# The FFN's first product by Strassen's seven products, its weight sums on GpSimd, and h kept in DRAM

## The chip, the cores and the metric

The kernel runs on one core of one Trainium2 chip. The metric is the device time of one execution in microseconds (us). One number counts: the median over the runs of a kernel. Nothing else runs on the core.

## The reference

One layer of a diffusion transformer on 1024 tokens of 1024 features, with 256 context tokens that only give starting states to the scans. Everything is float32.

```python
px = modulate(x, mx[0], mx[1]) @ w_in[l]                    # 1024 x 3840
...
mix_x = token_mixers(px, hg_x, s_f, s_b, *mix_args)
x_new = layer_norm(ALPHA * x + mx[2] * (mix_x @ w_out[l]), ln1_g[l], ln1_b[l])
ffn_x = conv_ffn(modulate(x_new, mx[3], mx[4]), ffn_up[l], ffn_conv_w[l], ffn_conv_b[l], ffn_down[l], rows)
x_new = layer_norm(ALPHA * x_new + mx[5] * ffn_x, ln2_g[l], ln2_b[l])

def conv_ffn(h, w_up, conv_w, conv_b, w_down, grid_rows):
    a, g = jnp.split(h @ w_up, 2, axis=-1)                  # 1024 x 1024 @ 1024 x 5632
    bsz, t, f = a.shape
    a = dwconv3x3(a.reshape(bsz, grid_rows, t // grid_rows, f), conv_w).reshape(bsz, t, f) + conv_b
    return (jax.nn.gelu(a, approximate=False) * g) @ w_down # 2816 x 1024
```

The change is in `h @ w_up` and in what stands around it. The tokens are a grid of 16 rows by 64 columns; `dwconv3x3` is a 3x3 filter with weights of its own for every feature, so it needs all 1024 tokens of a feature of `a`.

## The kernel before

**Matrix products.** Each float32 operand is split into a high part (rounded to float32r by a cast on ScalarE) and a low part (the exact rest, by a subtraction on VectorE): `split`, lines 82 and 83. A product of 128 by 128 by 512 is then three matmuls: high by high, low by high, high by low (`mm3`, lines 102 to 104). Weights are loaded from DRAM by SyncE's queue (SP) in pieces of 128x512 into a ring of four tiles `r` and are split up to 350 instructions ahead of the program's place (`AHEAD`, `load_split`).

**Stages.** Start-up, the token mixers (scan, short convolution, spatial gate), the output projection with the first layer norm (`out_proj`), `ffn_up`, `ffn_down` with the last layer norm. `modulate2` turns the normalised tiles of x_new feature-major: PE transposes into a PSUM bank (tile `psB`, line 933), ScalarE scales and shifts it in the bank (line 935), and `split` makes the high and low parts `x2`. The first half of the tokens is done while `out_proj` still runs. The second half (tiles 4 to 7) comes at the end of it, and `banks_up` lets the first three column blocks of `ffn_up` begin with the first half, so that these products cover the second half's preparation.

**ffn_up** runs over 22 blocks f of 128 features. Block f has two columns of `w_up`: the column f for `a` and the column 22+f for the gate `g`. `up_half` computes 128 features by 512 tokens in one PSUM bank: 8 blocks of features, three matmuls each. So a column takes 48 matmuls and a block f 96. After the two halves of `a`, ScalarE writes the middle tap with the bias (line 953) and a copy of `a` (line 954) to SBUF; VectorE adds the other eight taps, one `scalar_tensor_tensor` each on all 1024 tokens (line 964); ScalarE applies Gelu in place (line 966); VectorE multiplies by the two banks of `g` (line 970). The result `h[f]` stays in SBUF for all 22 blocks, in the tiles `hk` (blocks 0 to 9, room that the scan used) and `h`. In blocks 2 to 9 one column of the last modulation is computed besides (`ada_col`), from which the row `gate5` is made.

**ffn_down** takes two halves of 512 tokens. For each, 22 blocks f of h are split again into high and low parts (`dh`; `dhr` for the first) and multiplied with rows f of `w_down` into all eight PSUM banks.

**What sets the order.** A scheduler puts each engine's instructions into one fixed list, by the program's order and the priorities (`high_priority`). An engine takes its list strictly in turn: an instruction that waits for a semaphore holds up all that stands behind it on its engine. SP's list holds the DMA starts in the same way. GpSimd (POOL) has eight instructions in the whole kernel, all at the start.

## Time and profile before

| | |
|---|---|
| time, median of 2 runs (1353.05 and 1355.92) | 1354.49 us |
| profiled execution: span from first to last instruction | 1354.2 us |
| TensorE busy (PE) | 1319.4 us, 6730 matmuls |
| VectorE busy (DVE) | 945.0 us, 1735 instructions |
| ScalarE busy (ACT) | 472.1 us, 878 instructions |
| GpSimd busy (POOL) | 1.7 us, 8 instructions |
| mean clock granted to TensorE | 0.997 |

For the profiled execution the record holds the span alone, and it lies 0.3 us under the median; the span is taken as the execution's own time. An engine's row gives its busy time, its share of the span and the number of instructions. In a group of instructions stand the line, the engine, the operation, output<-inputs, the shapes, the count, then the busy time in us and the mean in ns of one, then the idle time of the engine just ahead of these instructions with what ended it. In a timeline row stand the start and the length in us. Matmuls overlap in the record: each is listed with 0.39 us though the next begins about 0.23 us later, so the spacing of the starts is what one costs.

### The profile page before, as it was taken

The numbers are of one execution on the slowest core, as the hardware profiler recorded it, in microseconds if no ns is written. First come the engines' busy times: TensorE is split into PE (matmuls) and PEld (weight loads), VectorE is DVE, ScalarE is ACT, GpSimd is POOL, SyncE is SP. The second block draws the span as 40 slices with busy tenths as digits, with TensorE's granted clock in tenths as the row PEclk, the third lists the DMA queues.
The fourth block names the chain that finished last, engine by engine and source line by source line (L and its number), as shares of the span: only waits on it lengthen the run. The fifth ranks groups of instructions, "written<-read, shape, count | busy, mean of one in ns | idle before, by whom it ended". The sixth has DMA issues, their size and how long they took to land.

```text
span 1354.2 us, 17543 instructions
## 1 busy us (share of the span) xinstructions
PE 1319.4 (97%) x6730; PEld 1114.1 (82%) x6730; DVE 945.0 (70%) x1735; ACT 472.1 (35%) x878; POOL 1.7 (0%) x8
## 2 busy tenths in 40 slices
PE   4999999999999999999999999999999999999997
PEld 3888988898888887877888888888888888888885
DVE  7979954869688688886876757575656664349357
ACT  4744544433331424434322222222222233223330
POOL 0000000000000000000000000000000000000000
PEclk9999999999999999999999999999999999999998
DMA  9672410132131444221222111211111033235332
GB/s 331 249 242 77 133 63 31 32 116 81 40 112 60 137 148 156 99 104 62 95 77 78 63 63 47 68 50 54 47 47 47 31 115 135 93 109 201 111 105 82
DMA packets 60900, 135.14 MB, mean 100 GB/s; under 512 B 7168, under 2 KB 7824, under 8 KB 60816
## 3 DMA queue, kind: packets, MB, share of 16 engines
q1 hardware_dynamic: 60816, 134.02, 29.2%
q8 instruction: 53, 0.87, 0.3%
q14 instruction: 31, 0.25, 0.1%
HBM read 125.59 MB, written 8.40 MB: 99 GB/s over the span
## 4 chain that ended last, share of the span: by engine, by line
PE 82%; DVE 9%; DMA 4%; ACT 3%; issue 1%; DVEq 0%; SPq 0%; ACTq 0%
PE psA L102 16%; PE psA L103 16%; PE psA L104 16%; PE psB L103 9%; PE psB L102 9%; PE psB L104 9%; PE psB L575 4%; PE psB L614 1%; DMA r<-in_w_out 1%; DMA cada<-in_ada 1%; DVE adat L172 1%; ACT O L639 1%; DMA adat<-in_ada 1%; DVE bnst L137 1%; DVE wl L83 1%
## 5 line engine op out<-in xcount | busy, mean ns | idle before, releaser
L83 DVE TENSOR_TENSOR wl<-r,wh 128x512 fp32r<-128x512 f32 x160 | 104.3, 687 | 155.8 <-ACT wh L82 149.9
L82 ACT CAST wh<-r 128x512 fp32r<-128x512 f32 x160 | 92.5, 619 | 311.5 <-PE psB L103 160.7
L102 PE MATMUL psA<-x,wh 128*128 128x512 f32 x352 | 137.3, 390 | 0.8 <-ACT x L82 0.8
L104 PE MATMUL psA<-x,wl 128*128 128x512 f32 x352 | 137.2, 390 | 0.0
L103 PE MATMUL psA<-x,wh 128*128 128x512 f32 x352 | 137.2, 390 | 0.0
L102 PE MATMUL psB<-x,wh 128*128 128x512 f32 x352 | 137.0, 389 | 0.0
L104 PE MATMUL psB<-x,wl 128*128 128x512 f32 x352 | 136.9, 389 | 0.0
L103 PE MATMUL psB<-x,wh 128*128 128x512 f32 x352 | 136.9, 389 | 0.0
L102 PE MATMUL psA<-xh,wh 128*128 128x512 f32 x320 | 126.7, 396 | 0.0
L103 PE MATMUL psA<-xl,wh 128*128 128x512 f32 x320 | 126.4, 395 | 0.0
L104 PE MATMUL psA<-xh,wl 128*128 128x512 f32 x320 | 125.8, 393 | 0.0
L964 DVE SCALAR_TENSOR_TENSOR h<-a,par,h 128x945 f32<-128x945 f32 (+2 forms) x96 | 117.4, 1223 | 7.1 <-ACT a L954 4.2
L964 DVE SCALAR_TENSOR_TENSOR hk<-a,par,hk 128x945 f32<-128x945 f32 (+2 forms) x80 | 97.6, 1223 | 5.6 <-ACT a L954 3.4
L102 PEld LDWEIGHTS psA<-x,wh 128*128 128x128 f32 x352 | 66.0, 188 | 14.7 <-ACT x L82 1.2
L102 PEld LDWEIGHTS psB<-x,wh 128*128 128x128 f32 x352 | 66.1, 188 | 13.9 <-DVE x L83 0.3
L103 PEld LDWEIGHTS psB<-x,wh 128*128 128x128 f32 x352 | 66.1, 188 | 13.8
L103 PEld LDWEIGHTS psA<-x,wh 128*128 128x128 f32 x352 | 66.1, 188 | 13.6
L104 PEld LDWEIGHTS psB<-x,wl 128*128 128x128 f32 x352 | 66.1, 188 | 13.6
L104 PEld LDWEIGHTS psA<-x,wl 128*128 128x128 f32 x352 | 66.1, 188 | 13.6
L104 PEld LDWEIGHTS psA<-xh,wl 128*128 128x128 f32 x320 | 60.2, 188 | 11.8
L103 PEld LDWEIGHTS psA<-xl,wh 128*128 128x128 f32 x320 | 60.2, 188 | 11.8 <-issue 0.2
L102 PEld LDWEIGHTS psA<-xh,wh 128*128 128x128 f32 x320 | 60.2, 188 | 11.7 <-issue 0.2
(316 smaller groups left out, 2787.7 us busy)
## 6 DMA issues: line engine op xcount, KB each, us to landing
r<-in_wup SPq DMA_DIRECT2D x88, 256.0 KB, 2.7
r<-in_w_down SPq DMA_DIRECT2D x88, 256.0 KB, 2.9
r<-in_win SPq DMA_DIRECT2D x56, 256.0 KB, 2.8
ada<-in_ada SPq DMA_DIRECT2D x24, 512.0 KB, 3.8
adat<-in_ada SPq DMA_DIRECT2D x16, 512.0 KB, 6.7
r<-in_ada SPq DMA_DIRECT2D x26, 256.0 KB, 3.0
cada<-in_ada SPq DMA_DIRECT2D x11, 512.0 KB, 5.4
x<-in_x SPq DMA_DIRECT2D x8, 512.0 KB, 5.8
```

The costliest lines, as they stand in the source:

```text
L82: nc.scalar.copy(hi, src)
L83: nc.vector.tensor_tensor(out=lo, in0=src, in1=hi.bitcast(F32), op=ALU.subtract)
L102: mm(out, lh, rh, start=first, stop=False)
L103: mm(out, lh, rl, start=False, stop=False)
L104: mm(out, ll, rh, start=False, stop=last)
L137: nc.vector.bn_stats(out=st[:, c, :], in_=x[:, c * 512:(c + 1) * 512])
L172: nc.vector.tensor_tensor_reduce(out=t, in0=t, in1=sc[:, i * n:(i + 1) * n], scale=1.0, scalar=0.0 if i == 0 else acc[:, 0:1], op0=ALU.mul ...
L575: nc.tensor.matmul(b[:, c, :], A[:, t0:t0 + P], strided(kq, 3 * T + t0, [[2 * B, P // (2 * B)], [B - T, 2], [1, B]]), start=c == 0, stop=c ...
L614: nc.tensor.matmul(b[:, c, :], KTt[:, g * 4 + c, :], vt[:, g * 4 + c, hv], start=c == use[g][0], stop=c == use[g][-1])
L639: nc.scalar.activation(O[:, k, :], b[:, c, :], AF.Square, accum_out=ss[:, k:k + 1])
L964: nc.vector.scalar_tensor_tensor(out=o, in0=a3[:, r0 + di:r1 + di, c0 + dj:c1 + dj], scalar=cw(i, j), in1=o, op0=ALU.mult, op1=ALU.add)
```

## The change

**Seven products.** Let X be x2 transposed to features by tokens, cut into halves of features and of tokens, and for a block f let a11, a12 be the upper and lower feature halves of its `a` column and a21, a22 those of its gate column. The four results (a and g, each for both halves of the tokens) come from seven products of 128 by 512 by 512, not eight. Each is 4 blocks of features by three matmuls, so 12 matmuls. They use sums of weights, S1 = a21+a22, S2 = S1-a11, a12-S2, a11-a21, and sums of X, which are made once: the forms "11", "21", "22" are quarters of X, T1 to T4 are sums. Each form and each sum of weights is split into high and low parts of its own.

**Where the sums go.** `weight_form` makes the four sums and all seven low parts of a block on GpSimd, 11 operations of 128x512; the seven casts stay on ScalarE. The raw columns of a block come by two loads of 512 KB into tiles `raw`. Six pieces for the start come by `load_form`.

**A block's results.** Products 1, 6, 7 and 4 add up in one bank (`x`, tag B) and are read out in between: after 1 into `p1`, after 6 into `u2` (both ScalarE), after 7 with `r` on VectorE, after 4 by the multiplication with Gelu's result. Products 2, 5 and 3 go to a pair of neighbouring banks `zv` (tag A, now allotted as two pairs). VectorE adds p1 or u2 to a half of the pair (`a_done`), ScalarE writes the middle tap with the bias back into the bank, and the eight taps accumulate in the pair in PSUM, with `a` read from SBUF.

**Start.** `up_begin` begins blocks 0 to 3 with products of the first token half (72 matmuls: product 1 of blocks 0 to 3, product 2 of 0 and 1), then normalises tiles 4 to 7, transposes 32 pieces into the second halves of the two pairs, and makes the forms; "22" and T3 have their low parts on GpSimd. x_new's first half, modulated, was stored to DRAM (`xr`) and comes back for the sums. Blocks 0 and 1 then go together through products 6, 5, 3, 7, 4; blocks 2 and 3 through the rest of theirs; blocks from 4 on through all seven.

**h in DRAM.** Each block's h is stored to DRAM (`hd`), and `ffn_down` loads it again, 128x512 at a time, into a ring of six tiles `hr`, by SP's queue. The rows `gate5`, `ln2_g` and `ln2_b` are loaded for `ffn_down` too. Small constants and masks move to pools that are given back earlier, and the mixers and `out_proj`, which used single banks of tag A, now get halves of the pairs.

```diff
+    def pair(self):
+        return self.pp.tile([P, 2, 512], F32, tag="A", bufs=2, name=self.name("psA"))
+
     def bank(self, tag="A", shape=(512,)):
+        if tag == "A":
+            if self.half is None:
+                self.half = self.pair()
+                b = self.half[:, 0]
+            else:
+                b, self.half = self.half[:, 1], None
+            return b if len(shape) == 1 else b.rearrange("p (a b) -> p a b", a=shape[0])
         return self.pp.tile([P, *shape], F32, tag=tag, bufs=4, name=self.name("ps" + tag))
...
-    def split(self, src, hi, lo):
+    def split(self, src, hi, lo, on=None):
         nc = self.nc
         nc.scalar.copy(hi, src)
-        nc.vector.tensor_tensor(out=lo, in0=src, in1=hi.bitcast(F32), op=ALU.subtract)
+        (on or nc.vector).tensor_tensor(out=lo, in0=src, in1=hi.bitcast(F32), op=ALU.subtract)
...
+    FORM = {1: "11", 2: "21", 3: "22", 4: "T4", 5: "T1", 6: "T2", 7: "T3"}
...
+    def weight_form(self, u, k):
...
+            if k in (5, 6) and "S1" not in r:
+                r["S1"] = combine(self.Rt(nm="s1"), a21, a22, ALU.add)
+            if k == 6:
+                r["S2"] = combine(self.Rt(nm="s2"), r["S1"], a11, ALU.subtract)
+            if k == 3:
+                combine(a12, a12, r["S2"], ALU.subtract)
+            if k == 7:
+                combine(a21, a11, a21, ALU.subtract)
+            src = {1: a11, 2: a12, 3: a12, 4: a22, 5: r.get("S1"), 6: r.get("S2"), 7: a21}[k]
+            self.split(src, w[:, 0], w[:, 1], pool)
+        return w
+
+    def product(self, k, work):
+        for j in range(4):
+            xh, xl = self.form(self.FORM[k], j)
+            c = slice(j * P, (j + 1) * P)
+            for bank, w, start in work:
+                mm = self.nc.tensor.matmul
+                mm(bank, w[:, 0, c], xh, start=start and j == 0, stop=False, skip_group_check=True)
+                mm(bank, w[:, 0, c], xl, start=False, stop=False, skip_group_check=True)
+                mm(bank, w[:, 1, c], xh, start=False, stop=j == 3, skip_group_check=True)
+
+    def up_begin(self, ys):
...
+        self.product(1, [(us[0].x, w[0], True)])
+        self.product(2, [(us[0].zv[:, 0], w[1], True)])
+        self.product(1, [(us[1].x, w[2], True)])
+        self.product(2, [(us[1].zv[:, 0], w[3], True)])
+        self.product(1, [(us[2].x, w[4], True)])
+        self.product(1, [(us[3].x, w[5], True)])
+        self.norm2(ys)
...
+        def one(j):
+            raw, v, t2 = self.S((2, 512), nm="xraw"), self.S((2, 512), nm="xv"), self.Rt(nm="t2")
+            nc.sync.dma_start(raw, self.xr[j])
+            for i in range(2):
+                self.shift2(us[i].zv[:, 1], ys, j + 4 * i, v[:, i])
+            nc.vector.tensor_tensor(out=raw[:, 0], in0=v[:, 0], in1=raw[:, 0], op=ALU.subtract)
+            nc.vector.tensor_tensor(out=t2, in0=v[:, 1], in1=raw[:, 0], op=ALU.subtract)
+            self.split(t2, *self.form("T2", j))
+            held[j] = raw, v, t2
+
+        def two(j):
+            raw, v, t2 = held.pop(j)
+            self.split(raw[:, 0], *self.form("T1", j))
+            self.split(v[:, 1], *self.form("22", j), nc.gpsimd)
+            nc.vector.tensor_tensor(out=v[:, 0], in0=v[:, 1], in1=v[:, 0], op=ALU.subtract)
+            self.split(v[:, 0], *self.form("T3", j), nc.gpsimd)
+            nc.vector.tensor_tensor(out=raw[:, 1], in0=raw[:, 1], in1=t2, op=ALU.subtract)
+            self.split(raw[:, 1], *self.form("T4", j))
+
+        for f, j in ((one, 0), (one, 1), (two, 0), (one, 2), (two, 1), (one, 3), (two, 2), (two, 3)):
+            f(j)
+        self.begun = us[2:]
+        self.units(us[:2], (6, 5, 3, 7, 4))
...
+        def after(self, k):
...
+            def a_done(g, c):
+                z = self.zv[:, g]
+                nc.vector.tensor_tensor(out=self.a[:, g], in0=z, in1=c, op=ALU.add)
+                nc.scalar.activation(z, self.a[:, g], AF.Identity, scale=cw(1, 1), bias=b.par[:, C_CB + f:C_CB + f + 1])
+
+            if k == 6:
+                nc.scalar.copy(self.u2, self.x)
+                self.a = b.ut("a")
+                a_done(0, self.p1)
+            elif k == 5:
+                self.r = b.ut("r")
+                nc.scalar.copy(self.r[:, 0], self.zv[:, 1])
+            elif k == 3:
+                a_done(1, self.u2)
...
+                        nc.vector.scalar_tensor_tensor(out=o, in0=a3[:, r0 + di:r1 + di, c0 + dj:c1 + dj], scalar=cw(i, j), in1=o,
+                                                       op0=ALU.mult, op1=ALU.add)
+                self.h = b.ut("h")
+                nc.scalar.activation(self.h.rearrange("p g t -> p (g t)"), z, AF.Gelu)
+            elif k == 7:
+                nc.vector.tensor_tensor(out=self.r[:, 1], in0=self.x, in1=self.r[:, 0], op=ALU.add)
+            elif k == 4:
+                for g, m in ((0, self.x), (1, self.r[:, 1])):
+                    nc.vector.tensor_tensor(out=self.h[:, g], in0=self.h[:, g], in1=m, op=ALU.mult)
+                nc.sync.dma_start(b.hd[f], self.h.rearrange("p g t -> p (g t)"))
+
+    def units(self, us, ks):
+        for k in ks:
+            ws = [self.weight_form(u.f, k) for u in us]
+            self.product(k, [(u.open(k), w, k in (1, 2, 5)) for u, w in zip(us, ws)])
+            for u in us:
+                u.after(k)
...
-                with self.tc.high_priority((2 * self.AHEAD, 0, 0)[f] if g == 0 and f < 3 else self.AHEAD):
-                    self.split(self.h[f][:, g * 512:(g + 1) * 512], *hh)
+                with self.tc.high_priority(self.AHEAD):
+                    h = dn.tile([P, 512], F32, tag="hr", bufs=6, name=self.name("hr"))
+                    nc.sync.dma_start(h, self.hd[f][:, g * 512:(g + 1) * 512])
+                    self.split(h, *hh)
```

The fixed lists show the change at three places. GpSimd, where the first column block's weights are made: `x_` are low parts of the forms "22" and T3, `s_` and `raw_` the sums of weights of block 0, `wf_6041` the low part that its product 6 needs. Before, GpSimd had no instruction here.

```order
L95 TENSOR_TENSOR x_816_5775<-xv_5930,x_814_5773 128x512
L95 TENSOR_TENSOR x_820_5779<-xv_5930,x_818_5777 128x512
L95 TENSOR_TENSOR x_816_5775<-xv_5948,x_814_5773 128x512
L95 TENSOR_TENSOR x_820_5779<-xv_5948,x_818_5777 128x512
L95 TENSOR_TENSOR x_817_5776<-xv_5976,x_815_5774 128x512
L95 TENSOR_TENSOR x_821_5780<-xv_5976,x_819_5778 128x512
L997 TENSOR_TENSOR s_6046<-raw_6043 128x512
L997 TENSOR_TENSOR s_6048<-s_6046,raw_6042 128x512
L997 TENSOR_TENSOR raw_6043<-raw_6042,raw_6043 128x512
L997 TENSOR_TENSOR raw_6042<-raw_6042,s_6048 128x512
L95 TENSOR_TENSOR wf_6041<-s_6048,wf_6041 128x512
```

The sums of block 0 stand behind six low parts of forms, and the low part for product 6 behind all four sums.

VectorE, a block's convolution and what stands behind it. Before (one block; `wl` are low parts of weights, the two L970 rows the multiplications of the block ahead):

```order
L970 TENSOR_TENSOR hk_5899<-hk_5899,psB_6109 128x512
L970 TENSOR_TENSOR hk_5899<-hk_5899,psB_6134 128x512
L83 TENSOR_TENSOR wl_6388<-r_6389,wh_6387 128x512
L83 TENSOR_TENSOR wl_6388<-r_6393,wh_6387 128x512
L964 SCALAR_TENSOR_TENSOR hk_5899<-a_6169,par,hk_5899 128x15x63
L964 SCALAR_TENSOR_TENSOR hk_5899<-a_6169,par,hk_5899 128x960
```

And now, the end of blocks 0 and 1 (`psA_5783` and `psA_5784` are their pairs; L1122 is the addition of `r` after product 7, L1125 the multiplications after product 4):

```order
L1117 SCALAR_TENSOR_TENSOR psA_5783<-a_6092,par,psA_5783 128x15x63
L1117 SCALAR_TENSOR_TENSOR psA_5784<-a_6096,par,psA_5784 128x15x63
L1117 SCALAR_TENSOR_TENSOR psA_5783<-a_6092,par,psA_5783 128x960
L1117 SCALAR_TENSOR_TENSOR psA_5784<-a_6096,par,psA_5784 128x960
L1117 SCALAR_TENSOR_TENSOR psA_5783<-a_6092,par,psA_5783 128x15x63
L1117 SCALAR_TENSOR_TENSOR psA_5784<-a_6096,par,psA_5784 128x15x63
L1122 TENSOR_TENSOR r_6129<-psB_5785,r_6129 128x512
L1122 TENSOR_TENSOR r_6131<-psB_5786,r_6131 128x512
L1125 TENSOR_TENSOR h_6175<-h_6175,r_6129 128x512
L1125 TENSOR_TENSOR h_6187<-h_6187,r_6131 128x512
```

The sixteen taps of both blocks take turns, and the additions that read the banks after product 7 stand behind all of them.

SP, where `ffn_up` ends and `ffn_down` begins. Before:

```order
L97 DMA r_8823<-in_wup 128x512
L97 DMA r_8892<-in_wup 128x512
L97 DMA r_8896<-in_wup 128x512
L97 DMA r_8968<-in_w_down 128x512
L97 DMA r_8972<-in_w_down 128x512
L97 DMA r_9006<-in_w_down 128x512
```

And now (`hd_96` is the store of block 21's h, `hr_9123` the first load of block 0's):

```order
L109 DMA r_9113<-in_w_down 128x512
L109 DMA r_9117<-in_w_down 128x512
L1126 DMA hd_94<-h_8780 128x1024
L1126 DMA hd_95<-h_8921 128x1024
L1126 DMA hd_96<-h_9062 128x1024
L1190 DMA hr_9123<-hd_75 128x512
L1190 DMA hr_9162<-hd_76 128x512
```

The loads of h stand behind the last store. At the start of `ffn_up` the same queue holds the stores of blocks 0 and 1 ahead of the loads of the columns of blocks 2 and 3.

More of the change, by code (lines that the diff above doesn't have):

```diff
@@ L249, in consts, with form_tiles, form @@
+            with tc.tile_pool(name="down", bufs=1, **left) as dn:
+                self.ffn_down(dn)
+    def form_tiles(self, pool):
+        return [[pool.tile([P, 2, 512], F32R, name=self.name("x2_")) for _ in range(2)] for _ in range(2)]
+    def form(self, name, j):
+        return (self.X[name][p][j // 2][:, j % 2, :] for p in range(2))
     def consts(self):
@@ L986, in up_half, with shift2 @@
[L986 to L991 removed]
+    def shift2(self, tp, ys, kt, out):
+        nc = self.nc
+        for j, y in enumerate(ys):
+            nc.tensor.transpose(tp[:, j * P:(j + 1) * P], y[:, kt * P:(kt + 1) * P], self.ident)
+        nc.scalar.activation(out, tp[:, :len(ys) * P], AF.Identity, scale=self.mods[:, 32 + kt:33 + kt], bias=self.mods[:, 24 + kt:25 + kt])
```

205 lines of the change are left out of this document (116 added, 89 removed).

## The prediction

> **What bounds the kernel now.** First the page's busy times and the shares of the chain that ended last:
>
> ```profile
> span 1354.2 us, 17543 instructions
> PE 1319.4 (97%) x6730; PEld 1114.1 (82%) x6730; DVE 945.0 (70%) x1735; ACT 472.1 (35%) x878; POOL 1.7 (0%) x8
> PE 82%; DVE 9%; DMA 4%; ACT 3%; issue 1%; DVEq 0%; SPq 0%; ACTq 0%
> ```
>
> TensorE is the bound, and the question is whether it is so in each stage. The windows answer that (length, then PE, weight loads, DVE, ACT, POOL, each with its count):
>
> ```profile
> 100.00:600.00 500.00, 494.50 (x2985) 430.64 (x2984) 385.68 (x818) 195.17 (x412) 0.80 (x1) 1.00 0.28 92
> 600.00:640.00 40.00, 39.14 (x184) 31.09 (x183) 29.63 (x87) 15.76 (x35) 0.00 (x0) 1.00 0.21 78
> 660.00:1130.00 470.00, 470.00 (x2076) 389.05 (x2075) 311.63 (x355) 133.70 (x212) 0.00 (x0) 1.00 0.20 65
> 1130.00:1160.00 30.00, 30.00 (x134) 24.86 (x133) 9.77 (x16) 8.34 (x15) 0.00 (x0) 1.00 0.32 106
> ```
>
> From 660 to 1130 us, in `ffn_up`, PE never stops, and the clock granted is full. At the seam to `ffn_down` (1130 to 1160) it never stops either. So a matmul taken out there is worth its whole spacing, and each microsecond that PE waits for anything new is lost whole. The only waits around the stage's start are two, from the list of waits:
>
> ```profile
> PE psB L933 <- ACT ly L927: 0.9, 1, 0.9
> PE psA L102 <- ACT x L82: 0.8, 1, 0.8
> ```
>
> The spacing comes from PE's timeline, the same instruction one block apart:
>
> ```profile
> 703.01 0.39 PE L102 MATMUL psB<-x,wh 128*128 128x512 f32 x1
> ...
> 724.77 0.39 PE L102 MATMUL psB<-x,wh 128*128 128x512 f32 x1
> L102 PE MATMUL psA<-x,wh 128*128 128x512 f32 x352 | 137.3, 390 | 0.8 <-ACT x L82 0.8
> ```
>
> 21.76 us for 96 matmuls: 0.2267 us each. The group is one of six with 352: 2112 matmuls, 22 blocks of 96.
>
> **What goes.** 84 matmuls in place of 96 in 22 blocks: 264 x 0.2267 = 59.85 us. The two waits above (1.7 us) go too, since I count the start afresh. That leaves 1354.2 - 61.55 = 1292.65 us, to which the new waits are added.
>
> **A block in the steady run.** PE needs 84 x 0.2267 = 19.04 us. The other engines by these rows:
>
> ```profile
> L83 DVE TENSOR_TENSOR wl<-r,wh 128x512 fp32r<-128x512 f32 x160 | 104.3, 687 | 155.8 <-ACT wh L82 149.9
> L82 ACT CAST wh<-r 128x512 fp32r<-128x512 f32 x160 | 92.5, 619 | 311.5 <-PE psB L103 160.7
> 835.87 10.04 DVE L964 SCALAR_TENSOR_TENSOR hk<-a,par,hk 128x945 f32<-128x945 f32 x8 [0.38 <-ACT a L954]
> L970 DVE TENSOR_TENSOR h<-h,psB 128x512 f32<-128x512 f32 x24 | 15.4, 684 | 1.2 <-ACT h L966 1.2
> L966 ACT ACTIVATE h<-h 128x1024 f32<-128x1024 f32 x12 | 12.8, 1063 | 6.9 <-DVE h L964 6.9
> L954 ACT COPY a<-psA 128x512 f32<-128x512 f32 x44 | 25.6, 581 | 0.0
> L953 ACT ACTIVATE h<-psA,par 128x512 f32<-128x512 f32 x24 | 18.6, 776 | 34.8 <-PE psA L104 34.8
> L172 DVE CUSTOM_DVE_ANT_0 r<-r,gate,adaacc 128x512 f32<-128x512 f32 x8 | 6.0, 749 | 1.5 <-DMA r<-in_ada 1.3
> 1.01 0.29 POOL masks.py:199 TENSOR_SCALAR_AFFINE_SELECT ident<-ident 128x128 f32<-128x128 f32 x1
> 104.13 0.80 POOL L280 IOTA masktmp<- 128x128 int32 x1 [10.68 <-DVE masktmp L184]
> ```
>
> DVE: 10.04 for eight taps and five operations of 0.684, 13.5 us. ACT: 7 x 0.62 + 3 x 0.58 + 2 x 0.78 + 1.06 = 8.7 us. GpSimd: 11 operations for which no row exists. From below, the same subtraction takes 0.687 us on DVE. From above, four times the 128x128 rows are 1.16 us (the select, which reads and writes float32) and 3.2 us (the iota, which only makes integers). I take 1.16, the row that is nearest in kind: 12.8 us a block. GpSimd would become the bound above 19.04 / 11 = 1.73 us. The Trainium skill's "GPSIMD Engine Reference", section 3.1, has 4497 ns for an addition of 2048 float32 columns, which would be about 1.12 us for 512 (an estimate); with it the sum below is some 0.5 us less. No run so far shows the operation.
>
> So PE stays the bound between waits. Two waits recur. Product 4 needs product 7's bank read (0.68 us on DVE), and only 4 matmuls of the next block (0.9 us) stand between: 0.1 to 0.3 us a block. Product 5 writes the pair in which `a_done` of the other half works; that stands on DVE behind six taps of the block before. From product 3's end: 0.68 + 0.78 + 6 x 1.255 + 0.68 for product 7's reading, then 0.68 + 0.78, together 11.1 us. PE meanwhile has 54 matmuls, 12.2 us. The margin, near 1 us, is gone in the eight blocks that also carry a modulation column (two operations of 0.749 us before, the row of line 172). I put 8 us over the stage, between 0 and 20.
>
> **The start (S1).** The rows of before, from T = 621.36, where the last matmul of `out_proj` ends its slot:
>
> ```profile
> 621.36 0.39 PE L102 MATMUL psA<-x,wh 128*128 128x512 f32 x1
> 628.41 0.66 PE L933 MATMUL psB<-ident,ly 128*128 128x128 f32 x4
> 616.71 4.25 DVE L137 BATCH_NORM_STATS2 bnst<-ly 128x6 f32<-128x512 f32 x7
> 631.77 1.25 ACT L927 ACTIVATE ly<-ly,nmt,rst 128x1024 f32<-128x1024 f32 x1 [0.39 <-ACT hk L953]
> L935 ACT ACTIVATE psB<-psB,mods 128x512 f32<-128x512 f32 x8 | 5.9, 794 | 0.4 <-PE psB L933 0.4
> ```
>
> The last tile was normalised at T + 11.7. Six of the seven statistics that ran before T now stand on DVE behind the last tile's residual: 4.1 us and some small ones, so T + 17. The cover is 72 matmuls, 16.3 us. Then ACT works through its list: before the cast of block 0's S2 come 8 evictions of 0.794 and 18 casts of 0.62, 17.5 us. The high part for product 6 is there at T + 36, and the transposes, which share two banks with the evictions, have long ended. GpSimd's six low parts of forms keep pace and end near T + 33; four sums and the low part of S2 (the first quoted list) end at T + 39, and seven operations later, at T + 47, comes block 1's low part, for which the sixth matmul of the paired product 6 waits. The other 67 matmuls of products 6, 5 and 3 take 15.2 us: product 3 ends at T + 62.4. PE's work up to there is 144 matmuls and eight groups of transposes, 32.6 + 5.3 = 37.9. The wait is 24.5, with half a microsecond for the reading between products 25 us. At 0.69 us on GpSimd the same chain gives 19, at 1.73 it gives 32.
>
> **The first pair's product 4 (S2).** Product 4 adds to banks that DVE must first read after product 7, and those two additions stand behind sixteen taps (the second quoted list). From product 3's end: 0.68 + 0.78, sixteen taps of 1.2 (two chains taking turns, the row's 1.255 less its chaining), 0.68: 21.4 us. PE has product 7 for that, 24 matmuls, 5.4 us. Wait: 16 us, from 14.5 to 17.5.
>
> **Block 2's weights (S3).** Their loads stand in SP's queue behind the stores of h of blocks 0 and 1.
>
> ```profile
> r<-in_wup SPq DMA_DIRECT2D x88, 256.0 KB, 2.7
> r<-in_w_down SPq DMA_DIRECT2D x88, 256.0 KB, 2.9
> x<-in_x SPq DMA_DIRECT2D x8, 512.0 KB, 5.8
> 846.54 0.93 SPq L97 DMA_DIRECT2D r<-in_wup  x2
> ```
>
> From product 4's end: two multiplications 1.4, the issue of a transfer 0.5 (0.93 for two), a load of 512 KB between 2.7 and 5.8 (4.5 taken), cast 0.62, GpSimd 1.16: 8.2 us. Product 2 covers 2.7 us of what product 6 then needs (three of GpSimd's sums, a cast, a low part, 5.1): 2.4 more. Together 10.6, from 8 to 13.
>
> **Up to down (S4).** Before, the first high part of h was cast while the last blocks still ran. Now the loads of h stand behind the last store (the third list). From block 21's product 3: 1.46, eight taps with the addition after product 7 among them 10.04 + 0.8, Gelu 1.06, two multiplications 1.37, issue 0.5, load 2.9, cast 0.62, low part 0.69, and half a microsecond of hand-overs: 20. PE has products 7 and 4, 5.4 us. Wait: 14.5, from 12 to 18.
>
> The banks in pairs tie halves together in the mixers, where PE is 98.9% busy: 2 us, from 0 to 5. The stores of 22 x 512 KB and their loads hide at a DMA share of 0.20.
>
> **Sum.** 1292.65 + 25 + 16 + 10.6 + 14.5 + 8 + 2 = 1368.75, so 1369 us. The gain of 60 us is real and four seams take it back. The median lies 0.3 us from the span, which changes nothing. With all terms at their low ends the sum is 1346, at their high ends 1398.
>
> **Rivals.** *Faster: the seams are covered.* By 2% faster is under 1327.4 us; then all waits together must be under 34.8 us. S2 with S4 alone are 30.5, so S1 and S3 would both have to be nearly covered, at 1327. That can be if I misread what a wait stands for in two of the fixed lists. Against it: each is one engine's list, taken strictly in turn. It has 14%.
>
> *Slower: taps in PSUM.* No row shows DVE writing a bank. On ACT, in place in a bank costs 794 ns, beside 776 from a bank to SBUF. If a tap takes d longer, S2 grows by 16d, S4 by 8d, and the wait of product 5 by 6d in some twenty blocks less the margin left: 144d - 4. It decides from d = 0.12 us (1382); at d = 0.2 it is 1394. It has 15%.
>
> *Slower: GpSimd is the bound.* Above 1.73 us each 0.1 us costs 1.1 us in twenty blocks, 22 us, and S1 stands at 32 or more: at 1.8 us, 1369 + 7 + 15 = 1391. The iota's row speaks for it, the select's against. The Trainium skill's "SBUF — State Buffer", section "Who interferes with whom", says that a VectorE instruction with two inputs in SBUF contends with a GpSimd instruction that reads SBUF. The taps now have one input in a bank; only the forms at the start and a few operations a block fall under this. It has 11%.
>
> *The change doesn't do what it says:* the fixed lists hold 22 x 84 matmuls, but their spacing could grow; 2%, 1369 + 60 at worst.
>
> **Chances.** The forecast has 58%. A difference of 2% (27 us, so 1327.4 and 1381.6) is what a measurement of this kernel surely tells; faster 0.15, within 0.58, slower 0.27. The range reaches from 1335, half-way to the covered case, to 1396.
>
> **What would show it.** Step by step: PE's spacing stays 0.227 us and its instructions fall by 264; a GpSimd subtraction takes 1.0 to 1.3 us; PE's waits list has four long entries, the two or three of the first product 6 on ACT and GpSimd, product 4 on the DVE addition for 16 us, product 2 of block 2 on ACT or SP for about 8, and the first product of `ffn_down` on the cast of `dhr` for about 14; from block 4 on a block takes 19.0 to 19.7 us. It is wrong if the seams together are under 40 us, if blocks take 20 us or more, or if the clock falls where PE has waited.

## The result, and the profile after

The changed kernel takes **1411.95 us**, the median of 1411.74 and 1412.15, against 1354.49 us before: a ratio of **1.0419, with a 95% interval from 1.0384 to 1.0453**. It is slower by 57 us, where 15 (1369 us, range 1335 to 1396) had been forecast. The profiled execution has a span of 1409.9 us, 1.8 us under its time of 1411.74.

The page of the changed kernel, its span, busy times, the clock granted in 40 slices, and the engines' shares of the chain that ended last:

```profile
span 1409.9 us, 17494 instructions
PE 1291.0 (92%) x6466; PEld 1069.0 (76%) x6466; DVE 973.6 (69%) x1717; ACT 532.7 (38%) x978; POOL 339.6 (24%) x258
PEclk9999999999999999998677999999999989999999
PE 42%; DVE 6%; POOL 2%; DMA 2%; issue 1%; ACT 1%; DVEq 0%; SPq 0%; POOLq 0%; ACTq 0%
```

264 matmuls are gone, as many as the change was to take away, but PE's busy time fell by 28.4 us only, not by 60, and the span grew. In slices 19 to 22 and in slice 33 the clock stands under 0.9; before, only the last of the forty did. The list of waits of the changed kernel (who waited <- for whom: us in total, times, longest; a wait of 17.5 us in the start-up, the same before and after, is left out):

```profile
PE psB L1019 <- DVE r L1122: 18.3, 4, 15.0
PE psB L1019 <- ACT s L1087: 14.1, 1, 14.1
PE psA L114 <- ACT dhr L94: 13.8, 1, 13.8
PE psA L1019 <- ACT wf L94: 8.5, 1, 8.5
PE psB L1021 <- POOL wf L95: 6.5, 3, 2.7
PE psA L948 <- ACT xv L949: 5.8, 5, 2.5
PE psB L1019 <- ACT wf L94: 4.4, 1, 4.4
```

These are the four seams of the forecast, with nearly the same releasers: the start (14.1, 4.4, some on POOL, and 5.8 among the transposes; the 14.1 end with the copy of product 1's bank, which stands directly behind the cast of S2 on ScalarE), product 4 of the first pair (15.0; 16 forecast), product 2 of block 2 (8.5; 8.2 forecast) and the first product of `ffn_down` (13.8; 14.5 forecast). The windows, cut at these waits (length, then PE, weight loads, DVE, ACT, POOL with counts, clock, DMA share, GB/s), show where more was lost:

```profile
100.00:600.00 500.00, 486.31 (x2925) 420.49 (x2924) 371.60 (x779) 184.03 (x387) 0.23 (x1) 1.00 0.27 89
651.63:676.96 25.33, 5.42 (x34) 3.60 (x32) 23.70 (x24) 16.60 (x29) 15.70 (x10) 0.66 0.18 65
676.96:707.25 30.29, 22.01 (x75) 16.08 (x76) 10.00 (x8) 10.15 (x18) 23.21 (x17) 0.72 0.00 1
707.25:727.20 19.95, 4.92 (x22) 3.75 (x21) 19.78 (x20) 3.15 (x4) 0.00 (x0) 0.68 0.00 0
727.20:743.39 16.19, 7.70 (x24) 5.86 (x25) 3.29 (x5) 3.25 (x5) 0.00 (x0) 0.71 0.48 166
743.39:770.15 26.76, 20.89 (x64) 15.37 (x64) 7.85 (x10) 8.05 (x14) 26.61 (x20) 0.78 0.37 136
828.78:1141.41 312.63, 311.01 (x1342) 249.03 (x1341) 217.84 (x212) 130.03 (x206) 218.00 (x166) 1.00 0.23 76
1158.28:1400.90 242.62, 242.19 (x1056) 198.74 (x1056) 134.40 (x245) 75.58 (x137) 0.00 (x0) 0.99 0.53 177
```

`ffn_up` begins at 635.27, not at 621.36: the mixers already have 8 us less PE work in 500 (486.31 where the kernel before had 494.50). Product 3 of the first pair ends at 707.25, product 4 begins at 727.20, block 2's product 2 at 743.39, block 2's product 4 at 770.15, `ffn_down` at 1158.28. Between 743.39 and 770.15 GpSimd is busy in 26.61 of 26.76 us. From 828.78 on sixteen blocks take 312.63 us, 19.54 each at full clock, which lies in the forecast's 19.0 to 19.7.

Set against the steps of the forecast:

| step | forecast, us | measured, us | difference |
|---|---|---|---|
| start of `ffn_up` | 621.4 and 2 for the banks in pairs | 635.3 | +11.9 |
| from there to the end of product 3 (S1) | 62.4 | 72.0 | +9.6 |
| to product 4 (S2, with product 7) | 21.4 | 20.0 | -1.5 |
| to product 2 of block 2 (S3, with product 4) | 13.6 | 16.2 | +2.6 |
| to product 4 of block 2 (64 matmuls and 2.4) | 16.9 | 26.8 | +9.9 |
| to the end of the last block's product 4 | 368.9 | 374.3 | +5.4 |
| wait for `ffn_down` (S4) | 14.5 | 13.8 | -0.7 |
| `ffn_down` to the end | 248.5 | 251.6 | +3.1 |

The last block's product 4 ends where the wait of 13.83 us for `ffn_down` begins, 1144.45. The differences add up to 40.3 us, out of 41 between the forecast and the span. Three rows carry most of it: the start, S1, and block 2.

Two more readings of the changed kernel. The spacing of matmuls behind a wait (timeline of PE: start and length, then the idle time before):

```profile
727.20 0.79 PE L1019 MATMUL psB<-xk,wf 128*128 128x512 f32 x1 [15.03 <-DVE r L1122]
727.79 0.63 PE L1020 MATMUL psB<-x,wf 128*128 128x512 f32 x1
728.22 0.63 PE L1021 MATMUL psB<-xk,wf 128*128 128x512 f32 x1
```

The second and third start 0.43 us apart, not 0.227, and the window of 16.19 us that begins here grants 0.71: the clock is halved after the wait. And what DVE and GpSimd take at the start, alone and beside each other (rows of the two timelines; the last is a group):

```profile
661.53 0.68 DVE L95 TENSOR_TENSOR xk<-t,xk 128x512 fp32r<-128x512 f32 x1
673.50 1.75 DVE L1059 TENSOR_TENSOR xraw<-xraw,t 128x512 f32<-128x512 f32 x1
675.17 1.75 DVE L95 TENSOR_TENSOR xk<-t,xk 128x512 fp32r<-128x512 f32 x1
674.66 1.71 POOL L997 TENSOR_TENSOR raw<-raw,raw 128x512 f32<-128x512 f32 x1
676.34 1.73 POOL L997 TENSOR_TENSOR raw<-raw,s 128x512 f32<-128x512 f32 x1
687.65 1.26 POOL L997 TENSOR_TENSOR raw<-raw,s 128x512 f32<-128x512 f32 x1
L1117 DVE SCALAR_TENSOR_TENSOR psA<-a,par,psA 128x945 f32<-128x945 f32 (+2 forms) x176 | 214.1, 1224 | 5.2 <-ACT psA L1096 1.3
```

A subtraction of two SBUF tiles takes DVE 0.68 us alone and 1.75 us while GpSimd works; GpSimd goes from 1.26 to 1.7 us. Side by side, each engine starts one operation every 1.68 us. Alone, DVE starts one every 0.60 us and GpSimd one every 1.24, so one of each in turn would take 1.84, and both on DVE 1.20: beside a DVE with such work, GpSimd takes away more than it adds. A tap in PSUM costs what a tap in SBUF cost, 1.22 us.

### The profile page after: what moved, and what is told of

It is laid out like the page before. It is cut to its first block, busy times and chain, and to the rows that moved or that the text cites. A ratio compares the mean times of both kernels' runs of the same rounds, so it can differ in the third digit from the quotient of the medians.

```text
span 1409.9 us, 17494 instructions
## 1 busy us (share of the span) xinstructions
PE 1291.0 (92%) x6466; PEld 1069.0 (76%) x6466; DVE 973.6 (69%) x1717; ACT 532.7 (38%) x978; POOL 339.6 (24%) x258
## 4 chain that ended last, share of the span: by engine, by line
PE 42%; DVE 6%; POOL 2%; DMA 2%; issue 1%; ACT 1%; DVEq 0%; SPq 0%; POOLq 0%; ACTq 0%
PE psB L1019 5%; PE psB L1021 5%; PE psB L1020 5%; PE psA L1019 4%; PE psA L1020 4%; PE psA L1021 4%; PE psA L114 3%; PE psA L116 3%; PE psA L115 3%; DVE psA L1117 3%; PE psB L114 3%; PE psB L116 3%; PE psB L115 3%; POOL s L997 1%; POOL wf L95 1%
## 5 line engine op out<-in xcount | busy, mean ns | idle before, releaser
L1117 DVE SCALAR_TENSOR_TENSOR psA<-a,par,psA 128x945 f32<-128x945 f32 (+2 forms) x176 | 214.1, 1224 | 5.2 <-ACT psA L1096 1.3
L95 POOL TENSOR_TENSOR wf<-raw,wf 128x512 fp32r<-128x512 f32 x104 | 138.8, 1338 | 115.1 <-ACT wf L94 115.0
L94 ACT CAST wf<-raw 128x512 fp32r<-128x512 f32 x104 | 64.0, 618 | 147.8 <-PE psB L1021 100.5
L95 DVE TENSOR_TENSOR dwl<-r,dwh 128x512 fp32r<-128x512 f32 x80 | 52.4, 690 | 85.5 <-ACT dwh L94 85.1
L1019 PE MATMUL psB<-xk,wf 128*128 128x512 f32 x176 | 73.9, 420 | 36.7 <-DVE r L1122 18.3
L1020 PE MATMUL psB<-x,wf 128*128 128x512 f32 x264 | 104.1, 394 | 0.0
L1095 DVE TENSOR_TENSOR a<-psA,s 128x512 f32<-128x512 f32 x44 | 30.3, 690 | 92.5 <-PE psA L1021 92.5
L94 ACT CAST dwh<-r 128x512 fp32r<-128x512 f32 x80 | 46.6, 620 | 107.8 <-PE psB L116 80.6
L1019 PE MATMUL psA<-x,wf 128*128 128x512 f32 x176 | 72.3, 412 | 8.5 <-ACT wf L94 8.5
L1021 PE MATMUL psB<-xk,wf 128*128 128x512 f32 x176 | 71.8, 408 | 6.5 <-POOL wf L95 6.5
L94 ACT CAST wh<-r 128x512 fp32r<-128x512 f32 x72 | 42.0, 618 | 86.4 <-PE psA L115 59.0
L95 DVE TENSOR_TENSOR wl<-r,wh 128x512 fp32r<-128x512 f32 x72 | 47.5, 688 | 35.9 <-ACT wh L94 22.7
L1019 PE MATMUL psB<-x,wf 128*128 128x512 f32 x176 | 69.1, 392 | 3.0 <-ACT s L1099 3.0
L1020 PE MATMUL psA<-x,wf 128*128 128x512 f32 x176 | 69.9, 397 | 0.0
L1021 PE MATMUL psA<-x,wf 128*128 128x512 f32 x176 | 69.6, 395 | 0.2 <-POOL wf L95 0.2
L116 PEld LDWEIGHTS psA<-xh,wl 128*128 128x128 f32 x320 | 60.2, 188 | 12.3 <-DVE wl L95 0.5
```

The source lines that it names most:

```text
L94: nc.scalar.copy(hi, src)
L95: (on or nc.vector).tensor_tensor(out=lo, in0=src, in1=hi.bitcast(F32), op=ALU.subtract)
L116: mm(out, ll, rh, start=False, stop=last)
L1019: mm(bank, w[:, 0, c], xh, start=start and j == 0, stop=False, skip_group_check=True)
L1020: mm(bank, w[:, 0, c], xl, start=False, stop=False, skip_group_check=True)
L1021: mm(bank, w[:, 1, c], xh, start=False, stop=j == 3, skip_group_check=True)
```

## The experiments

Times are single runs unless an interval stands with them, and those of the kernel before on the same chips lay between 1353.7 and 1357.0; so differences of 3 us and less carry nothing, and the traces' own marks carry the argument.

**1. The pairs of banks alone.** The kernel before with nothing but the new allotment, `pair` and `bank` as the change has them:

```diff
+        return self.pp.tile([P, 2, 512], F32, tag="A", bufs=2, name=self.name("psA"))
...
+                b, self.half = self.half[:, 1], None
```

> The kernel before, with one thing of the change: banks of tag A are halves of two pairs. The changed kernel reaches ffn_up 13.9 us later than the kernel before (635.27 against 621.36), of which the forecast allowed 2. Theory 'pairs': two halves are given back only together, so the mixers and the output projection wait for banks; this kernel takes 1364 to 1369 us, and its first matmul of ffn_up starts 10 to 14 us later than before. Rival 'traffic': the delay comes from the other edits there (modulated tiles through the ring r with stores to DRAM, six early pieces of weights, constants in other pools); then 1353 to 1357 us and a start near 621.

Measured: 1386.31 us, 29 above the kernel before and above what either theory had. `ffn_up` begins at 641.17, 19.8 later than before; `ffn_up` takes 492.2 us (484.4 before) and `ffn_down` 251.1 (248.5 before). The window of the mixers:

```profile
100.00:600.00 500.00, 482.33 (x2894) 417.93 (x2895) 369.76 (x768) 186.16 (x387) 0.24 (x1) 0.99 0.28 91
```

No matmul was added, and PE does 12 us less of them in the same 500. The pairs cost far more than the 2 us I had put down. The 7.9 us of `ffn_up` and the 2.6 of `ffn_down` don't carry over: the changed kernel uses its pairs otherwise in `ffn_up`, and the 2.6 are for the larger part a wait of 1.4 us for DVE that it doesn't have.

**2. Single banks until `out_proj` has ended.** The changed kernel with four single banks of tag A for the mixers, and two pairs from `ffn_up` on:

```diff
     def bank(self, tag="A", shape=(512,)):
+        if tag == "A" and self.single:
+            return self.pa.tile([P, *shape], F32, tag="A", bufs=4, name=self.name("psA"))
```

> The changed kernel with single banks of tag A up to the end of the output projection and pairs from ffn_up on. The kernel before with pairs reached ffn_up 19.8 us later, the changed one 13.9. Theory: pairs alone delay the mixers, so ffn_up begins near 621 and not 635: 1394 to 1400 us. Rival: the smaller pools of the change take some of it, and ffn_up begins at 628 or later: 1404 to 1410 us.

Measured: 1400.00 us. The mixers are back, and `ffn_up` begins at 620.68:

```profile
100.00:600.00 500.00, 495.14 (x2982) 432.27 (x2983) 382.73 (x811) 191.20 (x405) 0.80 (x1) 1.00 0.27 90
```

The waits behind it stay (14.0, 4.4, 15.0, 7.2, 14.1 us). So of the 57 us the pairs cost 12 by the time, and 14.6 by the start of `ffn_up`, ahead of the stage that the change is about.

**3. No GpSimd at the start.** The low parts of "22" and T3 and the weights of blocks 0 and 1 go to DVE:

```diff
-        pool = self.nc.gpsimd
+        pool = self.nc.vector if u < 2 else self.nc.gpsimd
...
-            self.split(v[:, 1], *self.form("22", j), nc.gpsimd)
+            self.split(v[:, 1], *self.form("22", j))
...
-            self.split(v[:, 0], *self.form("T3", j), nc.gpsimd)
+            self.split(v[:, 0], *self.form("T3", j))
```

> The changed kernel with GpSimd left out at the start of ffn_up: the low parts of the forms '22' and T3 and all sums and low parts of blocks 0 and 1 go to VectorE. In the changed kernel VectorE's subtractions of two SBUF tiles take 0.68 us alone and 1.75 beside a GpSimd operation, and GpSimd's 1.27 alone and 1.7 beside them. Theory 'contention': 36 operations for the forms and 6 for product 6 then take 29 us, and product 3 of the first pair ends near 62 us after the start of ffn_up and not at 72: 1400 to 1405 us, all these operations near 0.69. Rival 'VectorE becomes the bound': the 58 operations stand in one list and the weights of product 6 come no earlier: 1409 to 1418 us.

Measured: 1396.72 us, 15 less, under both ranges. `ffn_up` begins at 635.92, as in the changed kernel. From the timeline of PE:

```profile
670.53 0.80 PE L1019 MATMUL psB<-xk,wf 128*128 128x512 f32 x1 [9.80 <-ACT wf L94]
```

Every such DVE operation takes 0.68 to 0.69 us, and though DVE now does GpSimd's work as well, product 6 begins 34.6 us after the start and not 41.7: GpSimd's part at the start costs 7.1 us, by its own longer operations and by what it does to DVE's; the run does not part the two. A further 6.6 us lie inside product 6, whose waits of 1.6, 4.4 and 2.3 us have become one of 1.7. The scheduler also gave product 7 a place ahead of products 5 and 3. With that, product 4's wait of 15.0 is gone, and block 2's product 2 waits 23.4 us instead of 8.5. The list of ScalarE there says why:

```profile
717.40 1.28 ACT L1120 ACT_TABLE_LOAD   x1 [16.47 <-DVE psA L1117]
718.69 1.94 ACT L1120 ACTIVATE h<-psA 128x1024 f32<-128x1024 f32 x2
725.42 1.07 ACT L1087 COPY s<-psB 128x512 f32<-128x512 f32 x2 [4.79 <-DMA hd<-h]
727.56 0.62 ACT L94 CAST wf<-raw 128x512 fp32r<-128x512 f32 x1 [1.07 <-DMA raw<-in_wup]
```

Block 2's casts stand behind both Gelus of the first pair, and these behind sixteen taps; then the stores of `h` and the loads come. The two waits belong to one chain.

**4. Product 7 ahead of product 3, alone.**

```diff
-        self.units(us[:2], (6, 5, 3, 7, 4))
+        self.units(us[:2], (6, 5, 7, 3, 4))
```

> The changed kernel with the first pair's products in the order 6, 5, 7, 3, 4 and not 6, 5, 3, 7, 4: the banks are read after product 7 ahead of the sixteen taps, so product 4 no longer waits 15.0 us for them. Theory 'the wait moves on': the stores of h of blocks 0 and 1 still come behind the taps, and the loads for block 2 stand behind these stores in the queue, so block 2's first wait grows from 8.5 us to 20 or more: 1405 to 1413 us. Rival 'a wait of its own': 15.0 us and the 2.3 us of half clock behind it go, 1392 to 1396 us.

Measured: 1410.22 us, and one wait in place of two (15.0 and 8.5 make 23.5):

```profile
PE psA L1019 <- ACT wf L94: 24.3, 1, 24.3
```

It confirms the one chain by the smallest edit, and shows why nothing is won. From the end of product 3 to block 2's product 2 it is 29.9 us (712.96 to 742.89) in place of 36.1, since product 4 no longer stands in the chain; but product 3, with which the chain begins, now stands behind the 24 matmuls of product 7, 5.4 us.

**5. An attempt on all of it.** Single banks, product 7 ahead of 3, the stores of `h` of blocks 0, 1, 20 and 21 on ScalarE's queue, and `h`, `a`, `r` given their tiles early:

```diff
-                nc.sync.dma_start(b.hd[f], self.h.rearrange("p g t -> p (g t)"))
+                (nc.scalar if f in (0, 1, 20, 21) else nc.sync).dma_start(b.hd[f], self.h.rearrange("p g t -> p (g t)"))
```

> As the kernel with single banks, and with three waits attacked at their causes: the first pair in the order 6, 5, 7, 3, 4; the stores of h of blocks 0, 1, 20 and 21 issued by ScalarE, so that loads no longer stand behind them in SP's queue; the tiles of ffn_up laid so that those of blocks 2 and 3 don't lie on h of blocks 0 and 1. If the three waits are what the forecast says, 15 and 2.3 go at the first pair, 8 to 12 at block 2, and 5 to 8 at the seam: 1360 to 1372 us. Rival 'they move': block 2 waits for the taps of blocks 0 and 1 in another way (VectorE's list has its own additions behind them), and the seam waits for the last Gelu's bank: 1380 to 1394 us.

Measured: 1395.16 us, 1.2 above the rival's range and far from the theory's. The wait of 15.0 is gone and the one at `ffn_down` fell from 13.8 to 9.3, but block 2's product 2 waits (list of waits, SP's timeline, and SP's own waits):

```profile
PE psA L1027 <- ACT wf L96: 22.2, 1, 22.2
647.07 76.87 SPq L999 DMA_DIRECT2D raw<-in_wup  x5
SPq L999 <- DVE h L1133: 74.2, 1, 74.2
```

The loads stand in SP's list from 647 to 724, and what lets them go is the multiplication behind product 4 (L1133), which reads the pair's `h` and `r`. Freed from the stores, the loads wait for buffers of the first pair itself; that it is the room of `r` I take from the order of the allotments, and the trace does not show it. The casts still stand behind the Gelus.

**6. The first pair's weights asked for early.** `weight_form` for products 6, 5 and 3 of blocks 0 and 1 ahead of the last normalisation:

```diff
+        self.made = {}
+        for u in us[:2]:
+            for k in (6, 5, 3):
+                self.made[u.f, k] = self.weight_form(u.f, k)
         self.norm2(ys)
```

> The changed kernel with the weight forms of products 6, 5 and 3 of blocks 0 and 1 asked for ahead of the second half's normalisation, so that GpSimd makes their twelve sums and low parts ahead of the low parts of the forms. Theory: the first pair's product 6 waits for ScalarE's list and GpSimd's sums, one behind the other; asked for early, product 3 ends near 47 us after the start of ffn_up and not at 72: 1386 to 1394 us. Rival 'ScalarE's list alone': the forms' casts and evictions take as long whatever comes ahead, and the casts of weights only move; then a gain under 8 us, 1404 to 1412 us.

Measured: 1405.56 us, the rival's range. The start's longest wait fell from 14.1 to 11.4, but product 6 began 46.6 us after the start of `ffn_up`, where 41.7 had been, because GpSimd now works beside the layer norm on DVE, among others:

```profile
644.30 2.25 DVE L866 SCALAR_TENSOR_TENSOR ly<-ly,rst,ln_b 128x1024 f32<-128x1024 f32 x1
```

In the changed kernel the same operation takes 1.27 us there. Contention follows GpSimd's work to where it is put. The gain comes behind that: with the low parts ready, product 6 runs without a further wait, and products 6, 5 and 3 take 18.8 us (680.55 to 699.36) in place of 30.3.

**7. The clock, by waits put into the kernel before.** In six blocks a chain of GpSimd operations holds the weights of the gate column back, so that PE waits; nothing else is added:

```diff
+GAPS = {9: 0, 11: 1, 13: 2, 15: 3, 17: 5, 19: 9}
...
+            self.nc.scalar.mul(j[:, 0:1], self.gap[:, 0:1], 0.0)
+            for _ in range(self.gap_n):
+                pool.tensor_tensor(out=j, in0=j, in1=j, op=ALU.subtract)
+            pool.tensor_tensor(out=u[0][:, 0, 0:1], in0=u[0][:, 0, 0:1].bitcast(F32), in1=j[:, 0:1], op=ALU.add)
```

> The kernel before, with PE made to wait ahead of the gate column of six blocks of ffn_up (9, 11, 13, 15, 17, 19): a chain of 0, 1, 2, 3, 5 and 9 GpSimd subtractions of 128x512 starts when the block's a column is done and ends in the weights of its gate column, to which it adds zero. At 1.3 us an operation and 0.9 for the ends, the waits are 0.9, 2.2, 3.5, 4.8, 7.4 and 12.6 us, 31.4 together. Theory 'clock': a wait of several us halves PE's clock for whole periods of 3.4 us, which last into the work behind it; each of the three or four long waits costs 1.7 to 3.4 us more than itself: 36 to 45 us above the kernel before. Rival 'a wait costs itself': the half clock falls into the waits alone: 29 to 34 us above.

Measured: 1428.53 us, 74.8 above the kernel before. The waits came out longer than planned, since a GpSimd operation took about 1.9 us beside DVE, so the ranges above don't apply as they stand, and the waits of the trace take their place (list of waits; PE behind the first and shortest wait):

```profile
PE psB L105 <- POOL wh L1003: 57.4, 6, 19.1
838.32 0.59 PE L105 MATMUL psB<-x,wh 128*128 128x512 f32 x1 [3.44 <-POOL wh L1003]
838.71 0.63 PE L106 MATMUL psB<-x,wh 128*128 128x512 f32 x1
839.14 0.63 PE L107 MATMUL psB<-x,wl 128*128 128x512 f32 x1
```

`ffn_up` lasts 555.3 us (622.48 to 1177.78) where it lasted 484.4. Of these 70.9 us more, 57.4 are the waits and 13.5 are not, and the matmuls behind each wait stand 0.43 us apart. (The rest of the 74.8 lies ahead of `ffn_up` and in the difference between runs.)

**8. The same waits, with PE kept at work.** 226 matmuls with zero weights fill them:

```diff
+FILL = {9: 11, 11: 19, 13: 27, 15: 36, 17: 53, 19: 80}
...
+        if tag == "B" and g == 0 and self.gap is not None:
+            for _ in range(FILL[self.gap_f]):
+                self.nc.tensor.matmul(b, strided(self.zero, 0, [[0, P]]), self.x2[0][0][0][:, 0, :], start=True, stop=True)
```

> The kernel before with the same six waits on a chain of GpSimd, but TensorE works through 11, 19, 27, 36, 53 and 80 matmuls with zero weights (0.227 us each, into a bank that the next product starts afresh) inside them, so that each wait itself falls to 1 to 2 us. Places, chains and everything behind them are the same as without the filling, whose time was 74.8 us above the kernel before with waits of 57.4 us. 'Clock': what goes beyond the waits comes from half-clock matmuls behind them; filled, they disappear, the time is 55 to 63 us above the kernel before, and the matmuls behind each gap stand 0.227 us apart. 'Late engines': what goes beyond the waits comes from DVE, ScalarE and GpSimd, which the chain holds up; then the filling changes nothing and the time is 70 to 78 us above.

Measured: 1413.65 us, 59.8 above the kernel before.

```profile
PE psB L106 <- POOL wh L1008: 5.2, 6, 1.0
1089.06 18.66 PE L1015 MATMUL psB<-x,zero 128*128 128x512 f32 x80
1108.35 0.50 PE L106 MATMUL psB<-x,wh 128*128 128x512 f32 x1 [0.63 <-POOL wh L1008]
1108.68 0.40 PE L107 MATMUL psB<-x,wh 128*128 128x512 f32 x1
1108.91 0.39 PE L108 MATMUL psB<-x,wl 128*128 128x512 f32 x1
```

From the second matmul behind the fill on the spacing is 0.23 us. `ffn_up` lasts 543.6 us (619.24 to 1162.87), 11.7 less than without the fill, though the gaps are about as long (226 x 0.2267 + 5.2 = 56.4 against 57.4): 'clock' holds. The other 3 of the 14.9 us between the two times lie ahead of `ffn_up`, where neither kernel has a gap. So a wait of 3.4 to 19 us costs about 2 us beyond itself where PE's own work comes next.

**9. The same remedy in the changed kernel.** Zero matmuls in its long waits:

```diff
-        self.units(us[:2], (6, 5, 3, 7, 4))
+        self.fill(52, us[2].x)
+        self.units(us[:2], (6, 5, 3, 7))
+        self.fill(56, us[2].x)
+        self.units(us[:2], (4,))
+        self.fill(36, us[3].x)
```

> The changed kernel with matmuls by a column of zeros put where PE waits: 84 among and behind the transposes, 24 inside the first pair's product 6, 66 ahead of its product 4, 36 ahead of block 2's product 2, 58 at the seam to ffn_down. They add nothing to the results and stand ahead of the waiting matmuls. Theory 'clock': the waits are as long as forecast, and the rest of the loss is matmuls at half clock behind them, 23 us of excess busy time in ffn_up and 1.6 in ffn_down; kept busy, PE keeps its clock: granted clock 0.99 or more, 1383 to 1393 us. Rival 'contention': the matmuls there are slow since GpSimd, DVE or the banks are in use; then they stay slow, 1408 to 1416 us. Second rival 'clock follows work, not activity': zeros don't count, the clock falls as before, 1408 to 1416 us with a clock near 0.97.

Measured: 1418.87 us, slower than without. The mean clock rose from 0.969 to 0.986, but product 7 of the first pair began at 707.66 (707.25 without) and block 2's product 2 at 742.58 (743.39). Behind that:

```profile
PE psB L1030 <- POOL wf L95: 8.2, 2, 5.3
PE psB L1028 <- DVE r L1136: 7.6, 3, 4.6
```

So up to block 2 keeping the clock wins next to nothing: the time there is set by other engines. The test is clean for products 7 and 4 (707.66 to 742.58 at a clock of 1.00), not for product 6, where the fill stood too late and 676 to 690 still has 0.63. Behind 743 the waits are others than without the fill, so the loss there is no measure of the clock, and its cause was not followed.

**10. Blocks 2 and 3 without GpSimd.** GpSimd is busy throughout block 2. Its work for blocks 2 and 3 goes to DVE:

```diff
-        pool = self.nc.gpsimd
+        pool = self.nc.vector if u in (2, 3) else self.nc.gpsimd
```

> The changed kernel with the sums and low parts of the weights of blocks 2 and 3 on DVE (20 operations that took 26.6 us on GpSimd, 13.6 us at 0.68 each). Everything up to block 2's product 2 at 743 us stays as it was, with its wait of 8.5 us. 'GpSimd sets the pace behind that wait': in the changed kernel it was busy in 26.6 of the 26.8 us that block 2 took; relieved, the stretch from block 2's product 2 to the first matmul of ffn_down falls from 414.9 to between 404 and 408 us, and the time to 1401 to 1405. 'The clock sets it': the matmuls behind the wait run at half clock as before, the stretch stays at 411 to 415, and the time is 1408 to 1412.

Measured: 1407.18 us, with block 2's product 2 at 745.16 (1.8 later, of which 1.2 ahead of `ffn_up`) and the first matmul of `ffn_down` at 1151.54: 406.4 us between them in place of 414.9. The wait ahead of it is still 8.2 us, and the waits on POOL in the stretch are gone. GpSimd set the pace there and costs 8.5 us, with the half clock that its waits bring. The total fell by 4.8 where 7 to 11 were expected and lies between the two ranges; `ffn_down` took 2.2 us more, for a reason not followed. The marks, not the total, carry the verdict.

**11. Experiments 2 and 3 together.**

> The edits of the two runs before it together: single banks until out_proj has ended, and no GpSimd work before block 2. 'The terms are separate' (banks move the start of ffn_up, contention at the start lengthens the stretch behind it): ffn_up starts at 620 to 622, product 3 of the first pair ends 62 to 64 us later, block 2's product 2 still waits 20 to 24 us for its casts on ScalarE, ffn_down waits 9 to 14; the gains of 11.9 and 15.2 us add up to 1382 to 1387. 'They overlap' (the start is set by one chain, and only the later of the two counts): the start of ffn_up moves, but the first product 6 then waits as much longer, and the time is 1394 to 1400.

Measured: 1383.33 us, 28.6 less than the changed kernel; 11.9 and 15.2 had been the single gains. `ffn_up` begins at 621.38 and product 6 35.9 us later. Block 2's wait stays:

```profile
PE psA L1027 <- ACT wf L96: 23.3, 1, 23.3
```

The two causes are separate; the waits at the seams are in both. With half of the loss back it is still 28 us slower than the kernel before, and no version tried beats it.

## Why the prediction was wrong, step by step

**Right.** The matmuls cost what they were to cost (264 fewer; a block in the steady run takes 19.54 us at full clock). All four seams are there, with the engines named. S2 (15.0 for 16), the part of S3 ahead of block 2's product 2 (8.5 for 8.2) and S4 (13.8 for 14.5) have their sizes. Taps in PSUM cost 1.22 us, so that rival fell. Two small readings were wrong and changed nothing: the last stage before began at 1105.72, so the seam lay in the window called `ffn_up` and not in 1130 to 1160 (PE stops in neither), and six of the seven statistics are 3.6 us by the row, not 4.1 (the last tile was normalised at T + 16.1, forecast T + 17).

**The step "banks in pairs: 2 us, from 0 to 5" failed most.** It measured 13.9 us at the start of `ffn_up` in the changed kernel, 19.8 in the kernel before, and single banks brought the start back to 620.68 (experiments 1 and 2). I had taken 98.9% of PE's time as a sign that a coarser release would be hidden. It says the opposite: with PE busy 98.9% of the time there was nothing to hide it in. That two halves are released as one is how the allotment is written. The waits for tag A between 100 and 600 us grew from 2.1 to 8.0 us in all, spread over nine rows of the list of waits; how each hangs on a pair was not followed.

**S1 was 9.6 us too small, since GpSimd's sums came late.** The forecast had block 1's low part at T + 47. In the changed kernel, with T = 635.27, the matmul that waits for it starts at T + 54.9, and product 3 ends 17.1 us later where 15.4 had been put, the first eight matmuls at half clock:

```profile
690.18 0.80 PE L1021 MATMUL psB<-xk,wf 128*128 128x512 f32 x1 [2.26 <-POOL wf L95]
```

I had GpSimd at 1.16 us beside a DVE at full pace. Its six low parts of forms ended at T + 36.1, 3 us late, behind casts that waited for DVE. The twelve operations after them took 18.8 us: 13.9 had been forecast, 14.9 would be GpSimd's pace alone, and the last 3.9 are DVE beside it. I had the rule before me, the Trainium skill's "SBUF — State Buffer", section "Who interferes with whom", and set it aside because few operations fall under it. The trace agrees with the rule: two-input DVE operations go from 0.68 to 1.75 us, taps with one input in a bank stay at 1.22. But the few operations are a chain of 20 us that PE waits for. The first matmul of product 6 began at T + 41.7 where T + 36 had been forecast, and at T + 34.6 with GpSimd idle (experiment 3).

**S3's "2.4 more" was 12.3.** I charged block 2 with the operations that product 6 needs. But GpSimd had nothing to do for 40 us, held up by the same casts, and then had the work of blocks 2 and 3 to make up: 20 operations in 26.6 us, one after the other, against 64 matmuls that take 14.5. PE's part of the 12.3 is waits of 2.7 us for POOL and 3.0 for a copy on ScalarE, which stands behind a cast that waited 8.1 us for GpSimd's sum; most of the rest is matmuls at half clock behind these waits and the one of 8.5. The rival "GpSimd is the bound" has its place here, at 1.33 us an operation, without reaching the 1.73 of its condition: an engine that is fast enough in the steady run is the bound after this interruption until its lead is back. Experiment 10 puts 8.5 us on it.

**The clock was taken as full, and that was wrong.** What I had named as a sign of error, a clock that falls where PE has waited, is in the trace: from 651.63 to 743.39 the windows grant 0.66 to 0.72. The Trainium skill's "TensorE: Matmul & The Clock Gate", section "What's actually happening", gives half speed after one idle window of about 3.4 us. The trace agrees with the half and with the length, but the window need not be idle. Windows of the changed kernel, cut where the clock changes:

```profile
748.47:751.88 3.41, 1.04 (x5) 0.52 (x3) 2.70 (x4) 2.06 (x5) 3.41 (x3) 1.00 0.01 4
751.88:755.29 3.41, 3.13 (x7) 2.48 (x8) 0.24 (x1) 0.83 (x2) 3.41 (x4) 0.50 0.02 5
758.71:762.12 3.41, 0.38 (x2) 0.18 (x2) 0.00 (x0) 1.33 (x3) 3.41 (x4) 1.00 0.80 271
762.12:765.53 3.41, 3.41 (x9) 2.67 (x10) 2.34 (x2) 0.78 (x2) 3.41 (x3) 0.50 0.09 36
```

PE was busy for 1.04 us of the first and 0.38 of the third, by waits of only 2.65 and 3.03 us, and the window behind each ran at half clock. In all thirteen traces, cut into windows of 3.41 us, the clock went from full to half 57 times, each time behind a window in which PE was busy for at most 0.50 of it (two such windows, with 0.47 and 0.50, left it full), and it came back behind one with at least 0.83.

As a cost the clock must be placed with care. In the kernel before, six waits cost 11.7 us through it. In the changed kernel the matmuls of `ffn_up` are 23 us too long by the windows (447.6 us busy between 635.27 and 1158.28, against 1848 x 0.2267 + 5.3), less by their spacing, since the last matmul ahead of each wait is listed at full length. Up to block 2 keeping the clock gave back 0.8 us. Most of this time is set by GpSimd, DVE or ScalarE, so it may not be added to the terms above. Behind the wait for `ffn_down`, where PE's own work comes next, the clock does count: ten matmuls take 3.7 us in place of 2.3, about half of the 3.1 us that `ffn_down` lost. How much of the 2.6 us at product 4 and of the rest behind block 2 is the clock's stays open. From block 2's product 4 to the last block's, PE took 13.4 us beyond 1592 matmuls at 0.2267, where 8 (0 to 20) had been put; that is the row of +5.4.

**S2 and S3 were counted as two terms.** Their sum was right, 26.6 for 23.5; but it is one chain of taps, Gelus, stores, loads and casts, and putting product 7 ahead of product 3 does not shorten the sum of its waits (experiments 3, 4, 5 and 11: 23.4, 24.3, 22.2, 23.3 us); no other order was tried.

So the part of the forecast that says a gain of 60 us is taken back by four seams was right, and 1369 became 1412 chiefly by three terms: a bank allotment that touched all stages ahead (2 for 13.9), and GpSimd's work twice, beside DVE at the start (S1, 9.6 short) and in arrears at block 2 (2.4 for 12.3).

## What to carry to other kernels

Here fewer products did not pay, in part because the sums that they need came from an engine without a lead: cost such work not only in its steady run but right after each wait that is common to PE and that engine, and beside what the neighbour engine does then. A change to a shared resource (two banks that become one tile) is to be costed in every stage that uses it, above all where PE is 98 to 99% busy. And when two waits stand on the same in-order lists, add up the chain once: a reordering can move the wait and keep its length, as it did here.
